# Stacked query tiles of two attention mixers: one split over all 128 rows and transfers, where before each half was split on its own rows

## The chip, the cores and the metric

One core of one Trainium2 chip runs the whole program. The metric is the device time of one execution in microseconds (us). The kernel before takes 2039.87 us (median of three runs, 2039.81 to 2040.88).

## What is computed

A trunk of two layers over 512 positions of width 1024. Each layer is: half a SwiGLU step, a mixer, half a SwiGLU step, and a gated per-layer input. All products are made in a split form: a float32 value x is written as hi + lo, where hi is x rounded to TensorE's float32r and lo = x - hi, and three products (hi hi, hi lo, lo hi) are summed.

The mixer of layer 0 is `ab`, that of layer 1 is `c`. Cut to what matters here:

```python
# layer 0: A = windowed attention, 12 heads on 4 key heads; B = dilated attention, 12 heads
oa, _ = banded_attention(rope(qa), rope(ka), va, 128, sink)
ob = dilated_attention(rope(qb), rope(kb), vb)
h = h + concat([oa, ob]) @ w_out
# layer 1: 16 heads over an 8 x 16 neighbourhood of a grid, with a learned bias
h = h + neighbourhood_attention(q, k, v, rpb) @ w_out
```

## The kernel before

**Layout.** Features lie on the 128 rows (partitions), positions on the 512 columns. Heads are 64 wide, so a chunk of 128 projected features holds two heads: `hf` 0 on rows 0 to 63 and `hf` 1 on rows 64 to 127. The tiles in question come from a pool `act` of 62 buffers of 128 x 512 (L59, L83).

**Stacked tiles.** So that one product sums over 128 rows where a head has only 64, each head gets a tile of its own: its hi part on its own 64 rows and its lo part on the other 64 (`stack_q`, L573), against a key tile that holds the key's hi part on both halves (`stack_k`, L585: ScalarE copies hi to the head's own rows, L592, SyncE's queue moves it to the other rows by a transfer within SBUF, L593, and the lo part goes to a second tile, `low`, L595). For queries, ScalarE copies the head's 64 rows (L580) and VectorE subtracts on the same 64 rows and writes the other 64 (L581): four instructions of 64 rows for a chunk of two heads, and no transfer.

**Mixer `ab`** (L753). Chunks of queries and keys are projected, rotated (`rope`, L710: VectorE at L727 and L728, then four accumulating transfers from GpSimd's queue, L731) and then stacked: six chunks `("aq", gp, j)` of A with gp 0 or 1, and two chunks `("bq", sp, 0)` of B. Scores are made at L744 (and L958 for the other groups of B), reduced at L745 and L962. **Mixer `c`** (L1061): `proj_q` (L1089) projects a chunk, scales it (L1100), stacks it, and then SyncE's queue moves the hi part of each head to a third kind of tile, `sel` (L1104); `proj_k` (L1106) follows with L1110 and `stack_k`; scores are made at L1168. The first score product of a head pair needs the stacked query, `sel`, the stacked key and `low`.

**Order of the work.** `weave` (L853) interleaves the attention steps with the projections in the order of the program text; the tile framework's planner then lays down a fixed order for each engine by program order, priorities and its own estimates. An engine, and SyncE's queue too, takes its instructions strictly in that order: a transfer that waits for its source holds back those behind it. On SyncE's queue lie the weight loads (L167), the bias loads of `c` (L1092) and the transfers named above. `split_chunk` (L877) is the plain split: hi on ScalarE (L150), lo on VectorE (L151), each over all 128 rows, into two tiles of `act`. Lines 150 and 151 belong to a helper that also splits weights (`wh`, `wl`) and transposed probabilities (`tmp`).

Of the kernel before, what the change touches and what calls it, by code (L numbers as in the profile page):

```python
# [9 lines left out]
F32 = mybir.dt.float32  # L10
F32R = mybir.dt.float32r
BF16 = mybir.dt.bfloat16
AF = mybir.ActivationFunctionType
ALU = mybir.AluOpType
# [34 lines left out]
class Trunk:  # L49
# [520 lines left out]
        self.mm_unit(p, u, self.xg, True, True)  # L570
        return p

    def stack_q(self, q):  # L573

        nc = self.nc
        out = []
        for hf in range(2):
            own, oth = slice(hf * HD, (hf + 1) * HD), slice((1 - hf) * HD, (2 - hf) * HD)
            t = self.act(F32R)
            nc.scalar.activation(t[own, :], q[own, :], AF.Copy)  # L580
            nc.vector.tensor_tensor(t[oth, :], q[own, :], t[own, :].bitcast(F32), op=ALU.subtract)  # L581
            out.append(t)
        return out

# [168 lines left out]
    def ab(self, k_next):  # L753
        nc, io = self.nc, self.io
# [23 lines left out]
        t = {}  # L778
# [4 lines left out]
        def stacked(key, i, kind, p=None):  # L783

            c = []

            def stack():
                if key[0][1] == "k":
                    low = self.lows()
                    t[key] = (self.stack_k(c[0], low), low)  # L790
                else:
                    t[key] = self.stack_q(c[0])

            return [(key + (0,), 1, lambda: c.append(self.rope(p or self.project(w[i]), kind))), (key, 0, stack)]

# [638 lines left out]
```

## Time and profile before

| | us |
|---|---|
| median of three runs | 2039.87 |
| the profiled execution | 2041.7 |
| its span, first to last instruction | 2039.8 |
| TensorE (PE) busy | 2018.5 (99%) |
| VectorE (DVE) busy | 1510.8 (74%) |
| ScalarE (ACT) busy | 1056.6 (52%) |
| GpSimd (POOL) busy | 269.2 (13%) |

The profiled execution is 1.8 us over the median. `ab`'s attention lies at about 390 to 625 us of the span, `c`'s at about 1405 to 1600 us. PE is TensorE's matmuls, PEld its weight loads, SPq SyncE's queue. A matmul's end is modelled: rows of neighbouring matmuls overlap, and the starts tell their pace.

### The profile page before, as it was taken

To read this page: it belongs to the slowest core of one execution; us is meant where nothing else is said; L and a number is where in the kernel's file an instruction comes from. 1 tells how busy PE (TensorE), PEld (TensorE's weight loads), DVE (VectorE), ACT (ScalarE), POOL (GpSimd) and SP (SyncE) were. 2 spreads that over 40 slices of the span, in tenths; PEclk is the share of its full clock that TensorE was granted. 3 is DMA by queue.
4 is the path that set the end of the run, shared out by engine and by line. 5 is a ranking of instruction groups with operands and counts; after the bars stand their busy time and mean duration, and the time that the engine had idled before them with its cause. 6 is when DMAs were issued, how large, how long until landed. Compare 5 with 4: busy or idle time off the path is not lost.

```text
span 2039.8 us, 33724 instructions
## 1 busy us (share of the span) xinstructions
PE 2018.5 (99%) x12862; PEld 1820.6 (89%) x12862; DVE 1510.8 (74%) x2575; ACT 1056.6 (52%) x1798; POOL 269.2 (13%) x306
## 2 busy tenths in 40 slices
PE   9999999999999999999999999999999999999998
PEld 6999988878888899988888999888888889998886
DVE  8888865598766888875568888755778688888554
ACT  6555543377644555553445555434666545555342
POOL 1100011342212110001211100021000111000111
PEclk9999999999999999999999999999999999999999
DMA  7776644543424477653545765545333446665451
GB/s 222 192 187 184 186 142 159 143 98 73 100 72 165 134 197 183 170 191 123 184 152 154 197 182 158 191 143 154 110 104 110 155 127 188 184 180 164 132 204 42
DMA packets 122354, 312.93 MB, mean 153 GB/s; under 512 B 23504, under 2 KB 31184, under 8 KB 122192
## 3 DMA queue, kind: packets, MB, share of 16 engines
q1 hardware_dynamic: 102336, 249.91, 37.6%
q0 software_dynamic: 19712, 60.83, 15.4%
q8 instruction: 101, 1.65, 0.3%
q14 instruction: 61, 0.50, 0.1%
q10 hardware_dynamic: 144, 0.04, 0.0%
HBM read 274.02 MB, written 25.66 MB: 147 GB/s over the span
## 4 chain that ended last, share of the span: by engine, by line
PE 90%; DVE 3%; DMA 2%; ACT 2%; issue 1%; POOL 1%; SPq 0%; DVEq 0%; POOLq 0%; ACTq 0%
PE mm L365 6%; PE mm L364 6%; PE mm L363 6%; PE mm L176 6%; PE mm L177 6%; PE mm L175 6%; PE mm L440 5%; PE mm L441 5%; PE mm L442 5%; PE sc L364 3%; PE sc L363 3%; PE sc L365 3%; PE sc L175 3%; PE sc L177 3%; PE sc L176 3%; PE ob L365 2%
## 5 line engine op out<-in xcount | busy, mean ns | idle before, releaser
L150 ACT ACTIVATE wh<-wr 128x1024 fp32r<-128x1024 f32 (+2 forms) x455 | 465.6, 1026 | 533.6 <-PE mm L441 162.6
L151 DVE TENSOR_TENSOR wl<-wr,wh 128x1024 fp32r<-128x1024 f32 (+2 forms) x455 | 538.3, 1187 | 193.5 <-ACT wh L150 189.9
L365 PE MATMUL mm<-act,wl 128*128 128x256 f32 x1088 | 307.9, 283 | 0.0
L364 PE MATMUL mm<-act,wh 128*128 128x256 f32 x1088 | 307.9, 283 | 0.0
L363 PE MATMUL mm<-act,wh 128*128 128x256 f32 x1088 | 307.9, 283 | 0.0
L175 PE MATMUL mm<-act,wh 128*128 128x512 f32 (+1 forms) x648 | 254.0, 393 | 1.0 <-ACT wh L150 0.5
L176 PE MATMUL mm<-act,wh 128*128 128x512 f32 (+1 forms) x648 | 254.1, 392 | 0.6 <-DVE act L202 0.6
L177 PE MATMUL mm<-act,wl 128*128 128x512 f32 (+1 forms) x648 | 253.7, 392 | 0.0
L364 PEld LDWEIGHTS mm<-act,wh 128*128 128x128 f32 x1088 | 208.8, 192 | 0.3
L363 PEld LDWEIGHTS mm<-act,wh 128*128 128x128 f32 x1088 | 208.9, 192 | 0.2
L365 PEld LDWEIGHTS mm<-act,wl 128*128 128x128 f32 x1088 | 208.9, 192 | 0.2
L440 PE MATMUL mm<-act,wh 128*128 128x512 f32 x512 | 199.4, 389 | 0.0
L441 PE MATMUL mm<-act,wh 128*128 128x512 f32 x512 | 199.4, 389 | 0.0
L442 PE MATMUL mm<-act,wl 128*128 128x512 f32 x512 | 199.2, 389 | 0.0
L150 ACT ACTIVATE act<-tmp 128x512 fp32r<-128x512 f32 (+1 forms) x204 | 113.9, 590 | 85.5 <-DVE tmp L524 36.8
L363 PE MATMUL sc<-act,wh 128*128 128x256 f32 x544 | 154.0, 283 | 0.0
L364 PE MATMUL sc<-act,wh 128*128 128x256 f32 x544 | 154.0, 283 | 0.0
L365 PE MATMUL sc<-act,wl 128*128 128x256 f32 x544 | 154.0, 283 | 0.0
L176 PEld LDWEIGHTS mm<-act,wh 128*128 128x128 f32 x648 | 122.2, 189 | 24.7 <-DVE act L202 2.0
L175 PEld LDWEIGHTS mm<-act,wh 128*128 128x128 f32 x648 | 122.2, 189 | 23.8 <-ACT wh L150 1.0
L177 PEld LDWEIGHTS mm<-act,wl 128*128 128x128 f32 x648 | 122.2, 189 | 22.0 <-DVE wl L151 0.2
L151 DVE TENSOR_TENSOR act<-tmp,act 128x512 fp32r<-128x512 f32 (+1 forms) x200 | 125.4, 641 | 10.4 <-ACT act L150 8.8
(225 smaller groups left out, 4431.7 us busy)
## 6 DMA issues: line engine op xcount, KB each, us to landing
wr<-in_gu_dram SPq DMA_DIRECT2D x176, 512.0 KB, 4.6
wr<-in_gu_dram POOLq DMA_DIRECT2D x68, 512.0 KB, 5.5
wr<-in_dn_dram SPq DMA_DIRECT2D x64, 512.0 KB, 3.9
rb<-in_gu_dram SPq DMA_DIRECT2D x68, 256.0 KB, 2.9
wr<-in_dn_dram SPq DMA_DIRECT2D x32, 384.0 KB, 3.3
wr<-in_qk_ab_dram SPq DMA_DIRECT2D x20, 512.0 KB, 3.5
inner<-tmp POOLq DMA_DIRECT2D x32, 256.0 KB, 3.1
tmp<-inner SPq DMA_DIRECT2D x32, 256.0 KB, 4.4
```

Source lines behind the costliest of these rows:

```text
L150: self.put(self.nc.scalar.activation(hi, src, AF.Copy))
L151: self.put((lo_eng or self.nc.vector).tensor_tensor(lo, src, hi.bitcast(F32), op=ALU.subtract))
L175: mm(out, stat[0], mov[0], start=start, stop=False)
L176: mm(out, stat[0], mov[1], start=False, stop=False)
L177: return mm(out, stat[1], mov[0], start=False, stop=stop)
L363: mm(out, w[0][:, c], xs[k][0][:, x], start=start and k == 0, stop=False, skip_group_check=True)
L364: mm(out, w[0][:, c], xs[k][1][:, x], start=False, stop=False, skip_group_check=True)
L365: mm(out, w[1][:, c], xs[k][0][:, x], start=False, stop=stop and k == half - 1, skip_group_check=True)
L440: mm(p, u[0][:, c], xh, start=start and j == 0, stop=False, skip_group_check=True)
L441: mm(p, u[0][:, c], xl, start=False, stop=False, skip_group_check=True)
L442: mm(p, u[1][:, c], xh, start=False, stop=s + j == NF - 1, skip_group_check=True)
```

## The change

`stack_q` gets a flag, which is true for all chunks except the three `("aq", 0, j)`. With it, the chunk is split once by `split_chunk` (lo on VectorE) into two tiles of 128 rows, and for each of its two heads two transfers on SyncE's queue put the head's 64 rows of hi on its own rows of the stacked tile and its 64 rows of lo on the other rows. It holds for 3 chunks of A, 2 of B and 8 of `c`.

```diff
-    def stack_q(self, q):
+    def stack_q(self, q, moved=True):
...
-        nc = self.nc
-        out = []
+        nc, out = self.nc, []
+        parts = self.split_chunk(q, nc.vector) if moved else None
         for hf in range(2):
             own, oth = slice(hf * HD, (hf + 1) * HD), slice((1 - hf) * HD, (2 - hf) * HD)
             t = self.act(F32R)
-            nc.scalar.activation(t[own, :], q[own, :], AF.Copy)
-            nc.vector.tensor_tensor(t[oth, :], q[own, :], t[own, :].bitcast(F32), op=ALU.subtract)
+            if moved:
+                for rows, x in zip((own, oth), parts):
+                    nc.sync.dma_start(t[rows, :].bitcast(F32), x[own, :].bitcast(F32))
+            else:
+                nc.scalar.activation(t[own, :], q[own, :], AF.Copy)
+                nc.vector.tensor_tensor(t[oth, :], q[own, :], t[own, :].bitcast(F32), op=ALU.subtract)
             out.append(t)
...
-                    t[key] = self.stack_q(c[0])
+
+                    t[key] = self.stack_q(c[0], key[:2] != ("aq", 0))
```

## Rows read from the trace of the kernel before

**Rows 1.** The page's first part: busy time of each engine over the span, its share, and its instructions.
```profile
PE 2018.5 (99%) x12862; PEld 1820.6 (89%) x12862; DVE 1510.8 (74%) x2575; ACT 1056.6 (52%) x1798; POOL 269.2 (13%) x306
```

**Rows 2.** Busy time by stretches: the stretch, its length, then busy us (and instructions) of PE, PEld, DVE, ACT and POOL, the granted clock, the mean share of the DMA engines, GB/s. Two stretches of A, then 200 us of each mixer.
```profile
420.00:440.00 20.00, 19.90 (x102) 16.55 (x102) 19.33 (x49) 14.48 (x35) 7.05 (x9) 1.00 0.61 127
440.00:460.00 20.00, 19.34 (x101) 15.29 (x100) 19.35 (x45) 14.53 (x32) 8.27 (x12) 1.00 0.45 93
...
400.00:600.00 200.00, 196.18 (x1170) 165.78 (x1169) 162.73 (x422) 134.63 (x333) 53.72 (x71) 0.99 0.41 87
1400.00:1600.00 200.00, 197.72 (x1228) 174.94 (x1228) 147.35 (x404) 124.59 (x277) 6.39 (x8) 1.00 0.35 101
```

**Rows 3.** The chain of work that ended last, 420 to 462 us, in order of time: start, us, engine, tile and line.
```profile
427.29 0.70 DVE act L581
...
428.27 0.69 DVE act L581
...
432.80 0.62 ACT act L580
...
433.44 0.63 ACT act L580
...
434.53 0.39 PE ob L673
...
445.15 0.69 DVE act L581
...
446.46 0.69 DVE act L581
...
457.58 0.24 PE sc L744 x2
```

**Rows 4.** Groups by line and shape, 400 to 600 us: busy us, mean ns of one, idle time before and what ended it.
```profile
L581 DVE TENSOR_TENSOR act<-act,act 64x512 fp32r<-64x512 f32 x14 | 9.6, 686 | 0.5
...
L580 ACT ACTIVATE act<-act 64x512 fp32r<-64x512 f32 x13 | 8.1, 623 | 0.2
...
L151 DVE TENSOR_TENSOR act<-act,act 128x512 fp32r<-128x512 f32 x7 | 4.8, 686 | 0.2
L150 ACT ACTIVATE act<-act 128x512 fp32r<-128x512 f32 x7 | 4.4, 622 | 0.0
```

**Rows 5.** The same view, 1400 to 1600 us.
```profile
L581 DVE TENSOR_TENSOR act<-tmp,act 64x512 fp32r<-64x512 f32 x16 | 11.3, 705 | 1.1 <-ACT act L580 0.7
...
L151 DVE TENSOR_TENSOR act<-act,act 128x512 fp32r<-128x512 f32 x8 | 5.4, 677 | 1.4 <-ACT act L150 1.4
```

**Rows 6.** DVE in order of time, 544 to 552 us.
```profile
547.68 0.69 DVE L581 TENSOR_TENSOR act<-act,act 64x512 fp32r<-64x512 f32 x1
548.40 0.56 DVE L745 CUSTOM_DVE_ANT_0 act<-sc,act 128x384 f32<-128x384 f32 x1
```

**Rows 7.** PE in order of time, 548 to 550 us; in brackets the idle time before and what ended it.
```profile
549.02 1.20 PE L958 MATMUL sc<-act,act 64*128 64x128 f32 x8 [0.24 <-DVE st_b L745]
```

**Rows 8.** The chain of work that ended last, 544 to 556 us.
```profile
554.64 0.43 PE mm L176
...
555.40 0.23 PE mm L175
```

**Rows 9.** The view of rows 2 for the four microseconds around rows 8.
```profile
552.00:556.00 4.00, 4.00 (x13) 3.24 (x13) 3.24 (x15) 1.57 (x6) 0.36 (x1) 0.60 0.29 112
```

**Rows 10.** DVE in order of time: the end of the scaling of the query chunks 2, 4 and 6 of `c` (start, us, three instructions together).
```profile
1445.93 0.81 DVE L1100 SCALAR_TENSOR_TENSOR tmp<-mm,R 128x256 f32<-128x256 f32 x3
...
1492.45 0.81 DVE L1100 SCALAR_TENSOR_TENSOR tmp<-mm,R 128x256 f32<-128x256 f32 x3
...
1538.85 0.81 DVE L1100 SCALAR_TENSOR_TENSOR tmp<-mm,R 128x256 f32<-128x256 f32 x3
```

**Rows 11.** SyncE's queue in order of time for the same three chunks: start of the issue, us that the issues took, line, transfer, count.
```profile
1451.23 1.12 SPq L593 DMA_DIRECT2D act<-act  x2
...
1493.95 1.12 SPq L1104 DMA_DIRECT2D act<-act  x2
1495.16 0.54 SPq L167 DMA_DIRECT2D wr<-in_v_c_dram  x1
1497.09 1.12 SPq L593 DMA_DIRECT2D act<-act  x2
...
1540.35 1.12 SPq L1104 DMA_DIRECT2D act<-act  x2
...
1543.49 1.12 SPq L593 DMA_DIRECT2D act<-act  x2
```

**Rows 12.** PE in order of time: the first scores of the head pairs 2, 4 and 6.
```profile
1454.18 0.40 PE L1168 MATMUL sc<-act,act 128*128 128x256 f32 x2
...
1500.73 0.36 PE L1168 MATMUL sc<-act,act 128*128 128x256 f32 x1 [0.29 <-DMA act<-act]
...
1546.68 0.28 PE L1168 MATMUL sc<-act,act 128*128 128x256 f32 x1
```

**Rows 13.** From the views of line 593 (24 transfers) and of line 1104 (16 transfers): us from issue to landing, 128 KB each.
```profile
DMA to landing us min/median/max: 2.2/2.3/5.1
...
DMA to landing us min/median/max: 2.2/2.2/2.3
```

**Rows 14.** The chain of work that ended last, 1380 to 1640 us: the key's transfer of chunk 4.
```profile
1497.09 3.50 DMA act<-act
```

## The prediction

> **What bounds the kernel now.** I read the page's engine part first: PE is busy 2018.5 us of a span of 2039.8 us [rows 1], so no other engine can bound the whole, and the change leaves PE's products as they are. What it can move is PE's waits, and only in the mixers, so I took the stretches next. In 200 us of `ab` PE is idle 200 - 196.18 = 3.8 us, in 200 us of `c` 200 - 197.72 = 2.3 us [rows 2]. These are lower bounds of what can be gained, since a matmul's modelled end hides short gaps, but they set the scale: some 6 us in 2040.
>
> Who is late differs. In A, from 420 to 460 us, DVE is busy 19.33 and 19.35 us of each 20 [rows 2], and the chain of waits runs through DVE rather than PE: the reader finds the subtractions of `stack_q` there four times (0.70, 0.69, 0.69 and 0.69 us) and its ScalarE copies twice (0.62 and 0.63 us), these just ahead of the product at 434.53 us [rows 3]. In `c` DVE and ACT are busy 147 and 125 us of 200 [rows 2], and the one wait I found beside the queries' path is that for the key's transfer [rows 12, 14].
>
> **The change part by part.**
>
> *The split.* A chunk costs today two copies of 623 ns on ACT and two subtractions of 686 ns on DVE, each over 64 rows; the same operations over 128 rows take 622 and 686 ns [rows 4]. So each changed chunk saves about 0.62 us of ACT and 0.69 us of DVE; in `c` the subtraction goes from 2 x 705 to 677 ns, 0.73 us [rows 5]. Over 5 chunks in `ab` that is 3.4 us of DVE and 3.1 us of ACT, over 8 in `c` 5.9 us of DVE.
>
> What of it lies on the path: in A two chunks have both subtractions on the chain, 2.77 us, of which half stays: 1.4 us gained. The third has both copies there, 1.25 us, half stays: 0.6 us. In B the second subtraction of the last chunk ends at 548.37 us, the score reduction that follows it starts at 548.40 us [rows 6], and PE waits 0.24 us for that reduction [rows 7]: with the subtraction gone, that wait goes, 0.2 us. Next late there is PE itself, so no more comes of it. Sum for `ab`: 2.2 us gained. The bounds: nothing, if the next wait lies right behind, and 3.4 us, if all of DVE's saving is handed on.
>
> In `c` I take nothing for the saved work: PE runs through its instructions while DVE and ACT have slack [rows 2]. The bound is the 2.3 us that PE is idle there.
>
> *The transfers in `ab`.* 5 x 4 = 20 transfers of 128 KB, each issued in about 0.56 us (a pair takes 1.12 us [rows 11]) and landed 2.2 to 2.3 us later, at most 5.1 us [rows 13]. The chunk ready at 428.96 us is first used by the fourth pair of heads, whose scores are running at 457.58 us [rows 3]; four issues and one landing, 2.2 + 2.3 = 4.5 us, or 7.3 us with the longest landing, are covered by more than 20 us. Cost nothing. If that cover were gone, it would be those 4.5 to 7.3 us once for each of five chunks. What is queued behind the waiting transfers on SyncE's queue are weight loads; I price that at nothing in `ab`, from zero to the 2.3 us of one landing.
>
> *The transfers in `c`.* Here the path is short, and this is the cost. Take T as the end of the scaling of chunk 4: 1492.45 + 0.81 = 1493.26 us [rows 10]. Today the two `sel` transfers are issued from T + 0.69 on, a weight load follows at 1495.16 (T + 1.90), and the queue is free at T + 2.4; the key's first transfer becomes issuable at 1497.09 = T + 3.83 [rows 11], and the head pair's first score product starts at 1500.73 = T + 7.47, 0.29 us late, waiting for that transfer [rows 12], which took 3.50 us [rows 14]. With the change the queue has six transfers for the queries, each a pace of 0.6 to 0.65 us (1495.16 - 1493.95 = 1.21 for two), from the end of the hi copy at T + 0.69: until T + 4.5. The two `sel` transfers must also wait for a landing: T + 0.69 + 2.2 = T + 2.9, which is inside that time. With the weight load, 0.6 us, the queue is free at T + 5.1. So the key's first transfer, needed at T + 3.83, goes out 0.7 us late if the weight load is laid behind it, 1.3 us late if not; PE, already waiting there, loses all of it. Chunk 6 has the same distance (1543.49 - 1539.66 = 3.83 us), its scores start at 1546.68, and a landing of 2.3 us after 1543.49 leaves 0.9 us of slack: it loses 0 to 0.4 us. Chunk 2 has 1451.23 - 1446.74 = 4.49 us and 1454.18 - 1453.53 = 0.65 us of slack [rows 10 to 12]: 0 us. The other chunks have a longer distance to their key and I charge them nothing. Sum: 0.7 to 1.7 us lost, and I take 1.0 us, nearer the lower end, since the planner can lay the weight load behind the key.
>
> *Buffers and data.* Each changed chunk holds two more of the 62 `act` tiles for a few microseconds. By my count from the code `c` fills about 45 of 62, and `ab` is fuller; a wait there would fall on chunks that are used much later, so nothing, with the 2.3 to 5.1 us of a landing as the other end for one chunk. 13 x 4 x 128 KB = 6.8 MB are added to DMA engines that are busy 0.41 and 0.35 of the time [rows 2]: nothing.
>
> *A rule that speaks against it.* The pair of transfers that `stack_k` issues 0.6 us apart, each on 64 rows, land 2.2 to 2.3 us after their own issue at the median [rows 13], so their landings are no further apart than their issues. The Trainium skill (DMA: Bandwidth & Descriptors, Rules for kernel authors) says that two transfers to disjoint halves of the partitions serialize, and to use one of 128 partitions instead. If that held for the whole transfer, the six would take 6 x 2.2 us, and the sum would be that of the serial rival below; the rows speak for overlapped ones.
>
> **The sum.** -2.2 + 1.0 = -1.2 us. The profiled execution takes 2041.7 us around its span of 2039.8 us, so it would become 2040.5; against the median of 2039.87, which lies 1.8 us lower, 2038.7 us.
>
> **The rivals.**
>
> *More comes through (faster).* At 552 to 556 us the granted clock averages 0.60, between its levels of 1.2 and 2.4 GHz [rows 9], and matmuls of 512 columns follow each other by 0.43 us instead of 0.23 us [rows 8]; about seven of them make 1.5 us. Just before lie score products of 64 rows and the wait of 0.24 us [rows 7]. If the shorter subtraction closes that wait and the clock stays up, and DVE's 3.4 us are all handed on, with nothing lost in `c`: -3.4 - 1.5 - 0.2 = -5.1 us, 2034.8 us. For it: DVE is full in A. Against: it needs both, and PE's visible idle time in `ab` is 3.8 us in all.
>
> *The queue holds back the keys (slower).* One mechanism: SyncE's queue takes the `sel` transfers only when the hi transfers have landed, and the key's transfers stand behind them. If landings in that bunch take 3.5 us, as chunk 4's key did [rows 14], rather than 2.2, the first `sel` goes out at T + 4.2, the second 0.65 later, the weight load ends at T + 5.5, and the key lands at T + 5.5 + 3.5 = T + 9.0, against scores at T + 7.0 to T + 7.5 [rows 12]: 1.5 to 2 us for each of chunks 2, 4 and 6, and by the same longer landings some 0.6 us for four more: about 8 us, less 1 us from `ab`: 2047 us. It decides from the point where the bunch's landings pass about 3 us. For it: that one key did take 3.5 us with a weight load in flight. Against: the sixteen `sel` transfers never took more than 2.3 us [rows 13].
>
> *Serial transfers.* If each 64-row transfer waited for the one before, the queries would be stacked at T + 0.7 + 13.2, the key would land at T + 16, and three heads alone would lose 8.6 to 9 us each: 26 us, 2065 us. The rows exclude nearly all of it.
>
> *It changes nothing that shows.* Other work of PE and the planner's new order take up what DVE saves and what the queue costs: 2039.9 us.
>
> **How the numbers follow.** A measurement of this kernel can tell about 0.2%, 4.1 us, from no change. Forecast (2038.7): 0.50. Nothing shows: 0.14. More comes through: 0.20. The queue holds back the keys: 0.13. Serial: 0.03. The first two lie within 0.2%, so same 0.64, faster 0.20, slower 0.16. The planner lays out every engine's order anew, which the trace of before can't show; that and the bounds above make the forecast's own range 2036 to 2042. The range for 8 in 10 reaches from the faster rival's price, 2034.8, to inside the slower one, 2044.5.
>
> **What would show it.** Right: in A, 420 to 460 us, one subtraction of 128 rows and about 0.68 us for each chunk, DVE's busy time there down by about 2 us, and PE's stretch shorter by as much; in `c`, the transfers of `stack_q` landing after 2.2 to 2.3 us, the key's transfer of chunks 4 and 6 issued about a microsecond later after T, and PE waiting some tenths longer for it. Wrong: landings above 3 us in `c` and PE waits for transfers at most head pairs (the slower rival), the granted clock at 1.00 throughout 540 to 560 us and a gain above 4 us (the faster one), or PE waits in `ab` for a weight load that stands behind a query's transfer.

## The result, and the profile after

The kernel after the change takes 2043.88 us (median of 22 executions, 2041.33 to 2045.64), the kernel before 2040.41 us (22 executions, 2039.81 to 2042.52). The ratio is 1.0014, with a 95% interval of 1.0008 to 1.0020: a little slower, and more than the measurement's spread. The forecast was a little faster.

In the kernel after, lines lie lower: the transfers of `stack_q` are line 583, the splits over all rows run on the helper's lines 150 and 151, a product with the transposes is 678 (before: 673), a V product 639 (634), rope 732 and 733 (727, 728), the rotation transfers 736 (731), the scores 749 (744), the key's transfer 598 (593), `sel` 1110 (1104), the scaling in `c` 1106 (1100). In the kernels of the experiments they shift by a few lines more; tile and engine tell what is meant.

The page's first part, which answers to [rows 1]:

```profile
PE 2016.1 (99%) x12862; PEld 1820.0 (89%) x12862; DVE 1501.2 (74%) x2562; ACT 1049.0 (51%) x1785; POOL 269.8 (13%) x306
```

DVE does 1510.8 - 1501.2 = 9.6 us less work than before and ACT 7.6 us less, as the split promised. PE's busy time fell by 2.4 us as well, though its products are the same: the profiled execution of before holds a stretch at half clock [rows 9], and this one does not (the same four microseconds):

```profile
552.00:556.00 4.00, 4.00 (x31) 3.40 (x29) 2.62 (x13) 2.36 (x9) 0.00 (x0) 1.00 0.86 215
```

So the two profiled executions can't be set against each other by their ends: that of after is its shortest (2041.33 us, span 2039.5), that of before (2041.7 us) lies above its median. What can be compared is where PE waits. First the stretches of [rows 2]:

```profile
420.00:440.00 20.00, 17.61 (x91) 14.79 (x90) 16.26 (x45) 11.54 (x30) 6.41 (x9) 1.00 0.73 172
440.00:460.00 20.00, 19.67 (x100) 15.46 (x99) 16.76 (x37) 13.60 (x30) 7.33 (x10) 1.00 0.53 107
400.00:600.00 200.00, 192.86 (x1163) 163.69 (x1162) 158.16 (x417) 129.81 (x323) 53.84 (x70) 1.00 0.45 100
1400.00:1600.00 200.00, 199.20 (x1237) 176.43 (x1236) 142.82 (x397) 120.22 (x269) 7.52 (x9) 1.00 0.45 124
```

PE is idle 7.1 us of 200 in `ab` where it was 3.8, and 0.8 us in `c` where it was 2.3. In A, from 420 to 440 us, DVE is busy 16.3 us and no longer 19.3, yet PE is idle 2.4 us and no longer 0.1. The view of PE's waits names them (what PE waited for: us in total, times, longest). Before, 380 to 640 us, the four longest:

```profile
PE sc L744 <- DVE st_a L745: 0.9, 1, 0.9
PE tr L663 <- DVE act L933: 0.8, 2, 0.6
PE mm L634 <- DVE act L728: 0.6, 1, 0.6
PE sc L744 <- DVE st_b L745: 0.5, 1, 0.5
```

After, the same stretch:

```profile
PE ob L678 <- ACT tmp L150: 2.4, 1, 2.4
PE mm L639 <- DVE act L733: 2.1, 2, 1.5
PE sc L749 <- DVE st_a L750: 0.8, 1, 0.8
PE sc L749 <- DVE st_b L750: 0.5, 1, 0.5
```

Two waits of more than 1 us are new, both in A. All rows of this view come to 3.8 us before and 7.5 us after.

**The first wait** ends at 435.80 us. ACT, in order of time:

```profile
431.50 0.38 ACT L150 ACTIVATE tmp<-tr 128x256 fp32r<-128x256 f32 x1 [0.49 <-PE tr L668]
434.74 0.63 ACT L150 ACTIVATE act<-act 128x512 fp32r<-128x512 f32 x1 [2.86 <-DMA act<-tmp]
435.28 0.47 ACT L150 ACTIVATE tmp<-tr 128x384 fp32r<-128x384 f32 x1
```

The middle row is the new split of a chunk over all rows. It stands in ACT's order ahead of the copy that PE waits for, and ACT sits idle 2.86 us before it, because one of the chunk's four rotation transfers has not landed. The chain of waits has that transfer:

```profile
427.01 1.50 POOL act L736 x2
428.51 6.12 DMA act<-tmp
...
434.74 0.63 ACT act L150
435.37 0.38 ACT tmp L150
```

6.12 us for 64 KB. The same four transfers in the kernel before were issued from 427.65 to 429.15 us and landed so (issue to landing):

```profile
DMA to landing us min/median/max: 2.4/3.0/3.4
```

There ACT came to its two 64-row copies at 432.80 us [rows 3], when all of them had landed, the last at 432.53. SyncE's queue of the kernel after (start, us that the issues took):

```profile
425.09 0.33 SPq L167 DMA_DIRECT2D wr<-in_v_ab_dram  x1
425.64 3.81 SPq L583 DMA_DIRECT2D act<-act  x4
429.55 0.53 SPq L167 DMA_DIRECT2D wr<-in_v_ab_dram  x1
```

Four stacking transfers of 128 KB, and behind them a weight load of 512 KB, issued 1.04 us after the last rotation transfer. Before, that load went out at 431.10 us, 1.95 us after it. Ahead of each of the two loads DVE ends a subtraction from the buffers of the weights, first before, then after:

```profile
429.82 1.22 DVE L151 TENSOR_TENSOR wl<-wr,wh 128x1024 fp32r<-128x1024 f32 x1
```
```profile
427.26 1.22 DVE L151 TENSOR_TENSOR wl<-wr,wh 128x1024 fp32r<-128x1024 f32 x1
```

**The second wait** ends at 475.63 us. PE and then DVE, in order of time:

```profile
475.63 0.39 PE L639 MATMUL mm<-wh,act 128*128 128x256 f32 x1 [1.47 <-DVE act L733]
```
```profile
472.37 0.42 DVE L151 TENSOR_TENSOR tmp<-tr,tmp 128x256 fp32r<-128x256 f32 x1 [0.88 <-ACT tmp L150]
472.71 1.99 DVE L732 TENSOR_TENSOR tmp<-mm,act 128x512 f32<-128x512 f32 x2
474.53 1.04 DVE L733 TENSOR_TENSOR act<-mm,act 128x512 f32<-128x512 f32 x1
```

PE wants a PSUM bank for the V projection. Rope's products (732, 733) still read it, since they stand in DVE's order behind the low part of a transpose that PE made late. Before, the same products came at 469.44 and 471.28 us and V started at 472.59 without a wait.

**In `c`** the view of PE's waits has these rows before, 1400 to 1640 us:

```profile
PE ob L673 <- ACT tmp L150: 1.7, 7, 0.3
PE tr L223 <- DVE ssq L216: 0.3, 1, 0.3
PE sc L1168 <- DMA act<-act: 0.3, 1, 0.3
```

and this one after:

```profile
PE ob L678 <- ACT tmp L150: 0.8, 4, 0.2
```

The change gains there: the wait for the key's transfer is gone, and the copies of the transposes come to PE sooner. SyncE's queue behaved much as forecast, chunk 4:

```profile
1494.49 2.65 SPq L583 DMA_DIRECT2D act<-act  x4
1497.25 1.98 SPq L1110 DMA_DIRECT2D act<-act  x1
1499.32 0.55 SPq L598 DMA_DIRECT2D act<-act  x1
```

The scaling of that chunk ends at T = 1493.80 us (1492.98 + 0.82), so the key's first transfer goes out at T + 5.5, 1.7 us later than before [rows 10, 11] (forecast: T + 5.1). But the head pair's first scores stand at 1502.93 us, T + 9.1 and no longer T + 7.47: PE does other work first, and waits for nothing. The stacking transfers land after these times, in `c` and then in `ab` (issue to landing):

```profile
DMA to landing us min/median/max: 2.2/2.3/4.2
```
```profile
DMA to landing us min/median/max: 2.2/3.6/5.1
```

### The profile page after: what moved, and what is told of

The parts are those of the page before. It is cut to its first block, busy times and chain, and to the rows that moved or that the text cites. A ratio compares the mean times of both kernels' runs of the same rounds, so it can differ in the third digit from the quotient of the medians.

```text
span 2039.5 us, 33803 instructions
## 1 busy us (share of the span) xinstructions
PE 2016.1 (99%) x12862; PEld 1820.0 (89%) x12862; DVE 1501.2 (74%) x2562; ACT 1049.0 (51%) x1785; POOL 269.8 (13%) x306
## 4 chain that ended last, share of the span: by engine, by line
PE 74%; DVE 2%; ACT 2%; DMA 1%; issue 1%; POOL 1%; SPq 0%; DVEq 0%; POOLq 0%; ACTq 0%
PE mm L176 6%; PE mm L175 6%; PE mm L177 5%; PE mm L365 5%; PE mm L364 5%; PE mm L363 5%; PE mm L440 4%; PE mm L441 4%; PE mm L442 4%; PE sc L365 2%; PE sc L364 2%; PE sc L363 2%; PE sc L175 2%; PE sc L177 2%; PE sc L176 2%; PE mm L639 1%
## 5 line engine op out<-in xcount | busy, mean ns | idle before, releaser
L150 ACT ACTIVATE act<-tmp 128x512 fp32r<-128x512 f32 (+1 forms) x212 | 118.9, 592 | 89.0 <-DVE tmp L524 35.3
L151 DVE TENSOR_TENSOR act<-tmp,act 128x512 fp32r<-128x512 f32 (+1 forms) x208 | 131.4, 645 | 11.2 <-ACT act L150 9.7
```

The source lines that it names most:

```text
L150: self.put(self.nc.scalar.activation(hi, src, AF.Copy))
L151: self.put((lo_eng or self.nc.vector).tensor_tensor(lo, src, hi.bitcast(F32), op=ALU.subtract))
```

## The experiments

Theory one: `c` gains, A loses, and A's loss is the two waits. Theory two, from the slower rival: `c`'s key queue loses, and A/B gain. Four kernels ran beside the kernel before (2041.15 us, 29 executions).

**again** is the changed kernel without an edit.

> The changed kernel once more, unaltered, beside its parts on one chip. Its 22 runs lay between 2041.3 and 2045.6 us, and its one profile shows the fastest of them, with no stretch at half clock around 550 us. Theory 1 (the loss is two waits of PE in A, at 436 and 476 us, and in most runs a stretch at half clock behind them): again about 2043.9 us, and a profile of a slower run shows the same two waits and a mean granted clock below 1.00 somewhere in 380 to 640 us. Theory 2 (the loss is in c, keys held back behind the queries' transfers): the two waits in A cost nothing that the time shows, and a slower run shows longer waits for transfers at the scores of c.

2043.44 us, ratio 1.0011 (1.0002 to 1.0020). Of the executions at a mean granted clock of 0.998, five of this kernel average 2043.1 us and twenty of the kernel before 2040.8 us: 2.3 us apart. PE's waits differ by about as much: in `ab` and `c` they are 3.8 + 2.3 us before, 7.5 + 0.8 us in the changed kernel's first profile and 8.2 + 0.8 us in this one, so 2.2 and 2.9 us more. The first wait is 3.3 us here, where it was 2.4: with the same order on every engine its size changes from one execution to the next.

**c_only, b_only, a_only** keep the change in one stage:

```diff
-                    t[key] = self.stack_q(c[0], key[:2] != ("aq", 0))
+                    t[key] = self.stack_q(c[0], False)
...
-            qk["q", hp] = self.stack_q(q)
+            qk["q", hp] = self.stack_q(q, False)
```

The first edit alone is c_only. The other two have the second edit, and in place of the first `key[0] == "bq"` (b_only) or `key[:2] == ("aq", 1)` (a_only) as the second argument.

> Only the eight chunks of c take the transfers; all of A and B are split as before. Theory 1: faster than before by 1 to 2 us (2038.5 to 2039.5 us against 2040.4), as the trace after shows PE's excess in c smaller by 1.8 us. Theory 2: all of the loss, about 2043.5 us.

2038.97 us, ratio 0.9988 (0.9979 to 0.9997): faster.

> Only the two chunks of B take the transfers. Theory 1: within 1 us of before, 2039.5 to 2041.5 us, perhaps 1 us less if the wait at 549 us and the stretch at half clock behind it go. Theory 2: the same, 2040.4 us.

2039.52 us, ratio 0.9995 (0.9986 to 1.0004): no difference that shows.

> Only the three chunks of A with gp 1 take the transfers. Theory 1: the whole loss and more, 2043 to 2046 us, with PE waiting over 2 us near 436 us behind ScalarE, which waits for the last rotation transfer. Theory 2: no loss, 2038 to 2040.5 us.

2046.84 us, ratio 1.0027 (1.0016 to 1.0038): slower by 5.7 us, with both waits (3.0 and 1.9 us). In c_only, `c`'s waits are the same single row of 0.8 us as in the whole change, and neither of A's new waits is there. Theory two fell: the loss is all A's. The medians of a_only and c_only, +5.7 and -2.2 us, come to the +3.5 us of the whole change's first runs; beside these kernels, in again, it was +2.3.

That leaves A. Its change has two halves, the single split and the transfers, and each could delay the rotation or reorder the engines. Four kernels beside the kernel before (2040.34 us, 27 executions).

**bc**, the change without A:

```diff
-                    t[key] = self.stack_q(c[0], key[:2] != ("aq", 0))
+                    t[key] = self.stack_q(c[0], key[0] == "bq")
```

> The change kept in B and c and taken back in A (both groups of A split on 64 rows as before). If the parts add up, as measured singly (b_only 1.6 us under the kernel before, c_only 2.2 us under it), this is 3.8 us under the kernel before: a ratio of 0.998, no PE wait at 436 or 476 us, and PE idle in 1400:1640 near 0.8 us. If B and c gain through the same cover (or B's gain was only noise), it lies at 0.9985 to 0.999.

2038.03 us, ratio 0.9990 (0.9981 to 0.9999): 2.3 us under the kernel before, where the whole change was 2.3 and 3.5 us over it. It beats both. The parts add up to less than the 3.8 us hoped for: it is c_only's gain, and B adds nothing that shows.

**a_parts**, the single split without transfers, in A's second group alone; the two parts stand in for the stacked tiles:

```diff
...
+        if moved:
+            return self.split_chunk(q, nc.vector)
```

> Only A's second group changed, and of it only the split: one Copy and one subtraction over 128 rows, no transfers; the two parts stand in for the stacked tiles, so this group's scores are of other operands (work left out: the 12 transfers). The order on ACT still has the split of a chunk ahead of the copies of the transposes that PE waits for. If the loss of a_only (+5.7 us) is the order alone (a split that waits for all four rotations, ahead of work that PE needs), the waits at 436 and 476 us are here too, 2 to 3.5 us the first, and the time is 4 to 6 us over the kernel before. If it is the transfers beside the rotation, the four rotations land 2.5 to 3.4 us after their issue as before, the first wait is under 1 us, and the time is within 1.5 us of the kernel before or below it.

2042.42 us, ratio 1.0009 (1.0001 to 1.0018): 2.1 us slower. The four rotation transfers and the wait that came of them:

```profile
DMA to landing us min/median/max: 2.4/3.3/5.0
```
```profile
PE ob L675 <- ACT tmp L150: 1.3, 1, 1.3
```

This is neither expectation: the last rotation transfer takes 5.0 us though no stacking transfer is there.

**a_dummy**, the transfers without the single split, in A's second group alone: the 64-row split as before, and twelve transfers into tiles that nobody reads. The orders of ACT and POOL are those of the kernel before, DVE's all but the same; PE's has some small moves from 430 us on.

```diff
+        spare = [self.act(F32R), self.act(F32R)] if moved else None
...
             nc.vector.tensor_tensor(t[oth, :], q[own, :], t[own, :].bitcast(F32), op=ALU.subtract)
+            if moved:
+                for rows in (own, oth):
+                    nc.sync.dma_start(spare[hf][rows, :].bitcast(F32), t[rows, :].bitcast(F32))
```

> A as before (splits on 64 rows, stacked tiles complete by them), and beside it the same 12 transfers of 128 KB from SyncE's queue in A's second group, into spare tiles that nobody reads. ACT's, DVE's and POOL's orders are those of the kernel before. If the transfers are the loss, it is here: rotations that land 4 to 6 us after issue, a PE wait of 1.5 us or more near 435 us, 3 to 5 us over the kernel before. If the order is the loss, the time is within 1 us of the kernel before, though the rotations may land late.

2043.23 us, ratio 1.0013 (1.0005 to 1.0022): 2.9 us slower, and the first wait is there, 2.6 us, with the old order. Its chain of waits:

```profile
428.25 1.50 POOL act L735 x2
429.74 7.02 DMA act<-tmp
...
436.85 0.63 ACT act L581
```

This profile has one more wait that the kernel before lacks, 1.3 us at 399.9 us for the transfer of a key; it comes before the first of the twelve transfers, issued at 426.75 us, and so is none of their doing.

**a_pool**, a_only with the transfers on GpSimd's queue:

```diff
-                    nc.sync.dma_start(t[rows, :].bitcast(F32), x[own, :].bitcast(F32))
+                    nc.gpsimd.dma_start(t[rows, :].bitcast(F32), x[own, :].bitcast(F32))
```

> As a_only, with the 12 transfers issued on GpSimd's queue in place of SyncE's, so that no weight load stands behind them. In ACT's order the split of the second chunk now stands behind all four copies of the transposes. If the held weight loads or the split's place ahead of the copies is the loss, the first wait (436 us) is gone, and the time is 2 to 4 us under a_only; if the transfers' traffic beside the rotation is, it stays within 1 us of a_only. GpSimd's issues (about 0.5 us each by the rotation's rows) may also put the next rotation later.

2053.01 us, ratio 1.0063 (1.0051 to 1.0076). The first wait is gone, but the next rotation stands behind the stacking transfers on GpSimd's queue, PE waits 1.8 us and then 2.3 us for rope's products, and the clock falls to its lower level twice (the view of rows 2):

```profile
450.00:460.00 10.00, 8.69 (x37) 7.19 (x38) 5.88 (x13) 5.49 (x15) 8.18 (x12) 0.83 0.62 109
...
480.00:490.00 10.00, 9.46 (x56) 9.35 (x56) 7.27 (x27) 3.93 (x13) 6.29 (x8) 0.72 0.46 52
```

PE's waits in `ab` and `c` explain 4.5 us of the 12.7. At 709 us PE waits 2.0 us for ACT, where neither the kernel before nor a_only waits, and the clock falls a third time, from 711 to 715 us. The mean granted clock of its executions is 0.994, that of the kernel before beside it 0.998; at the lower level a product takes 0.43 us instead of 0.23 [rows 8], so an estimate for the clock is 0.004 x 2040 = 8 us. The three terms are more than enough for the 12.7 us. As a test of the load's queue it is worthless, since it changed too much.

**A third theory.** Put side by side, the slow rotations have one thing in common, and it is not the stacking transfers. The last rotation transfer of the chunk and the 512-KB weight load that follows it (us; landing as issue plus the landing time of the view by line):

| kernel | rotation issued, landed (took) | load issued, landed |
|---|---|---|
| before | 429.15, 432.53 (3.4) | 431.10, 434.8 |
| c_only | 428.76, 432.15 (3.4) | 430.71, 434.3 |
| b_only | 429.04, 432.41 (3.4) | 430.99, 434.6 |
| bc | 429.58, 432.98 (3.4) | 431.53, 435.3 |
| after | 428.51, 434.63 (6.1) | 429.55, 435.7 |
| again | 428.87, 435.92 (7.0) | 429.78, 435.7 |
| a_only | 432.33, 439.10 (6.8) | 433.30, 438.9 |
| a_parts | 431.70, 436.7 (5.0) | 432.56, 436.4 |
| a_dummy | 429.74, 436.77 (7.0) | 430.84, 436.6 |
| a_pool | 429.59, 434.94 (5.4) | 429.62, 434.4 |

Wherever in these rows the load is issued 1.1 us or less behind the rotation transfer, the transfer takes 5.0 to 7.0 us and lands from 1.1 us ahead of the load's end to 0.5 us behind it; where it is issued 1.95 us behind, the transfer takes 3.4 us, and no run lies between. a_parts has no stacking transfers, and in a_pool they are issued only after the load. So I held the load: a transfer of 512 B on SyncE's queue reads the rotated chunk, and the load is put behind it. All engines but SyncE keep their orders exactly. Four kernels beside the kernel before (2040.32 us, 33 executions).

```diff
+                    if key == ("aq", 1, 1):
+                        self.gate = nc.sync.dma_start(self.spare[96:, :], c[0][96:, 0:4])
...
-            u = self.unit(src[:, q * UNIT:(q + 1) * UNIT], lo_eng=self.lo_eng())
+            with self.tc.issue_after(self.gate.ins) if self.gate and not parts else ExitStack():
+                u = self.unit(src[:, q * UNIT:(q + 1) * UNIT], lo_eng=self.lo_eng())
+            if not parts:
+                self.gate = None
```

**whole_held**, on the whole change:

> The whole change, and one transfer of 512 B more on SyncE's queue, which reads the rotated second chunk of A's second group, so that the 512-KB weight load behind it is issued only when the rotation has landed; the orders of all engines are else those of the whole change. If that load, issued about a microsecond behind the last rotation transfer, is what makes this transfer land with it (434.64 against 435.71 us in the whole change, a_parts 436.66 against 436.43, a_dummy 436.77 against 436.59), the fourth rotation transfer lands within 4.3 us of its issue, the wait at 436 us falls from 2.4 us to under 0.7, and the kernel is 2 to 3 us faster than the whole change, so 2040.5 to 2041.5 here and within 0.1% of the kernel before. If the stacking transfers themselves are what slows the rotation, the wait stays over 2 us and the time at 2043 to 2044. The wait at 476 us stays in both cases.

2041.00 us, ratio 1.0003 (0.9994 to 1.0012). The rotation lands in 4.1 us at most, and the wait at 436 us falls from 2.4 us to 0.4:

```profile
DMA to landing us min/median/max: 3.0/4.0/4.1
```
```profile
PE ob L681 <- ACT tmp L150: 0.4, 1, 0.4
```

The hold moves the meeting to the next rotation, whose last transfer takes 9.4 us, and no longer 6.0 as in the kernel after. PE waits 1.5 us there, at 444 us (the second row), and the second wait stays (the first):

```profile
PE mm L642 <- DVE act L736: 2.1, 2, 1.5
PE ob L682 <- DVE tmp L151: 1.8, 2, 1.5
```

**a_parts_held**, on a_parts:

> a_parts (A's second group split over all rows, no transfers, other operands in its scores) with the same hold on the weight load. If the load is the cause, the fourth rotation transfer lands about 3.4 us after its issue as in the kernel before, not 5.0, the wait of 1.5 us near 437 us is gone, and the time is 1 to 2 us under a_parts, within 0.5 us of the kernel before or below it. If the split's standing for all four rotations is enough by itself, the wait stays at 1 us or more and the time at a_parts'.

2039.79 us, ratio 0.9997 (0.9988 to 1.0006), 2.6 us under a_parts, directly and against the kernels before beside the two. The wait is gone and the rotation lands as before:

```profile
DMA to landing us min/median/max: 2.4/3.0/3.4
```

**a_only_held**, on a_only:

> a_only with the same hold. If the load is the cause, the wait near 440 us falls from 3.2 us to under 0.7 and the time is 2.5 to 3 us under a_only, 2 to 3.5 us over the kernel before, of which 2.1 us is the wait at 480 us. If the stacking transfers are, it stays within 1 us of a_only.

2044.18 us, ratio 1.0020 (1.0011 to 1.0029), 2.7 us under a_only. Against the kernel before beside each, it is +3.9 where a_only was +5.7: 1.8 us less, short of the 2.5 expected, and over the 3.5 us that it was to stay within. The rotation lands in 4.4 us at most, the first wait is 0.6 us, the second stays at 1.9.

**before_held**, the control:

> The kernel before with the same hold: the control. Its load was issued 1.95 us after the last rotation transfer and 1.4 us ahead of its landing, so the hold puts it back by about 1.5 us. Both theories: within 0.5 us of the kernel before, no new PE wait.

2040.04 us, ratio 0.9998 (0.9989 to 1.0007), no new wait. The third theory holds for the first wait: in all three pairs it goes, or nearly, with the orders of PE, DVE, ACT and POOL untouched. In the times the intervals of each pair overlap, but all three fell against the kernel before, by 1.6 to 2.8 us (the whole change from +2.3 or +3.5 to +0.7). The load's place behind the rotation costs 1.6 us (a_parts) to 2.4 us (a_only: 6.8 against 4.4) of landing; with the stacking transfers and no load behind it, it takes 0.7 to 1.0 us longer than without them (4.1 and 4.4 us against 3.4). With the load held A still costs 3.9 us, and of the first wait only 0.6 us is left in that.

The second wait occurs in every kernel whose A has both the single split and the transfers (longest 1.5 us in after, again and whole_held, 1.9 in a_only and a_only_held, 2.3 in a_pool) and in none with one half alone (a_parts, a_dummy: 0.6 us, as before). To see whether it is the bank, ACT copies that projection, and no other, out and rope reads the copy (beside the kernel before at 2040.66 us, 27 executions).

```diff
+        if free:
+            own = self.act()
+            with self.tc.high_priority():
+                nc.scalar.activation(own, p, AF.Copy)
+            p = own
         o, u = self.act(), self.tmp()
```

**a_rope**, on a_only_held:

> a_only_held with one thing more: the bank of the projection whose rope products PE waited for at 476 us is copied out by ACT (one Copy of 128x512, about 0.6 us), and the rope products read the copy, so that PE's V projection no longer waits for DVE. If that bank is the second wait, it falls from 1.9 us to under 0.5 and the kernel is 1.5 to 2.5 us faster than a_only_held (2044.2), 1 to 2.5 us over the kernel before. If something else that comes with the transfers holds PE there, a wait of 1.5 us or more stays at that place and the time stays within 1 us of a_only_held.

2043.52 us, ratio 1.0015 (1.0006 to 1.0024). The wait is gone: the V projection starts like this in a_only_held and then in a_rope,

```profile
475.59 0.38 PE L642 MATMUL mm<-wh,act 128*128 128x256 f32 x1 [1.91 <-DVE act L736]
```
```profile
474.49 0.28 PE L642 MATMUL mm<-wh,act 128*128 128x256 f32 x1
```

but the time fell by only 0.7 us (1.0 against the kernels before beside the two), short of the 1.5 to 2.5 expected. The copy also changed the orders of PE, DVE and ACT, and other waits took the place of the one that went: those in `ab` come to 6.3 us, in a_only_held to 6.4.

**before_rope**, the control:

> The kernel before with the same copy on ACT, the control: its V projection started without a wait at 472.6 us, so there is nothing to win. Within 0.5 us of the kernel before, up to 1 us slower if ACT's 0.6 us falls on the chain.

2041.62 us, ratio 1.0004 (0.9995 to 1.0013). The copy itself brings a new order, with more waits for DVE: the rows of `ab` come to 6.0 us, not 3.8, led by

```profile
PE sc L749 <- DVE st_b L750: 1.8, 3, 0.7
PE tr L663 <- DVE act L938: 1.2, 2, 0.6
```

Against this control a_rope is 1.9 us slower, where a_only_held is 4.1 us slower than its own (before_held). That fits a second wait of about 2 us, but the edit was not clean enough to price it.

**whole_rope**, on whole_held:

> whole_held with the same copy: the whole change without both of its waits in A. If these two waits are all of the loss and c's 1.3 us and B's gain stay, it is 1.5 to 2 us under whole_held, at 2038.5 to 2039.5 us, on the faster side of the kernel before by 1 to 2 us, and no better than bc (2038.0). If the 1.6-us wait that whole_held has newly at 444 us (the next rotation beside the held load) stays as well, 2039.5 to 2040.5.

2040.05 us, ratio 0.9999 (0.9990 to 1.0008). The 1.4-us wait at 444 us stays. Without the second wait and with 0.4 us left of the first, the change is even with the kernel before, and bc is still the better kernel.

The sums of the view of PE's waits against the medians, each as the difference to the kernel before (waits: `ab` 3.8, `c` 2.3 us):

| kernel | waits in `ab` | in `c` | together, against before | median, against before |
|---|---|---|---|---|
| c_only | 3.6 | 0.8 | -1.7 | -2.2 |
| b_only | 4.0 | 1.7 | -0.4 | -1.6 |
| bc | 4.1 | 0.8 | -1.2 | -2.3 |
| after | 7.5 | 0.8 | +2.2 | +3.5 |
| again | 8.2 | 0.8 | +2.9 | +2.3 |
| a_only | 8.5 | 2.0 | +4.4 | +5.7 |
| a_parts | 5.5 | 2.2 | +1.6 | +2.1 |
| a_dummy | 6.6 | 1.7 | +2.2 | +2.9 |
| a_parts_held | 4.4 | 1.9 | +0.2 | -0.5 |
| a_only_held | 6.4 | 2.2 | +2.5 | +3.9 |
| whole_held | 6.5 | 0.8 | +1.2 | +0.7 |
| before_held | 3.7 | 2.2 | -0.2 | -0.3 |
| a_rope | 6.3 | 2.0 | +2.2 | +2.9 |
| before_rope | 6.0 | 2.7 | +2.6 | +1.0 |
| whole_rope | 5.8 | 1.1 | +0.8 | -0.6 |
| a_pool | 8.5 | 2.1 | +4.5 | +12.7 |

Without a_pool they agree within about 1.6 us. That is as large as some of the differences, so the table ranks the kernels and does not price each wait.

## Why the prediction was wrong

**The step that failed: "The transfers in `ab` ... Cost nothing", and with it "What is queued behind the waiting transfers on SyncE's queue are weight loads; I price that at nothing in `ab`".** I asked who waits for a load that comes late, and nobody does. I did not ask beside what a load runs that goes out at another moment. The load goes out after a subtraction on DVE that reads the buffers of the weights: that ended at 431.04 us before and ends at 428.48 us after, ahead of the rotation's last issue, and the four stacking transfers in the queue hold the load until 429.55. So it goes out 1.0 us behind the last rotation transfer and no longer 1.95, and that transfer lands after 6.1 us and not 3.4. ACT's split, which waits for it, stands ahead of a copy that PE needs: 2.4 us. The hold left 0.6 us or less of this wait and brought the medians, against the kernel before, from +3.5 (+2.3 in again) to +0.7 us (the whole change), from +2.1 to -0.5 (a_parts) and from +5.7 to +3.9 (a_only). The trace of before showed the mechanism already, one rotation further on, where nobody needed it: the four transfers issued from 433.2 to 434.7 us, beside a load issued at 434.41, took

```profile
DMA to landing us min/median/max: 2.4/5.8/6.3
```

In a_dummy, where the load after the same rotation goes out at 438.05 us, 2.5 us behind its last transfer, the four took 3.1 to 3.6 us.

"6.8 MB are added to DMA engines ... nothing" was wrong as well, by 0.7 to 1.0 us on the same landing.

**The order of the engines.** "The planner lays out every engine's order anew, which the trace of before can't show" stood among the uncertainties with no price of its own. With it came the second wait, 1.5 to 2 us. That PE waits there for rope's products is in the trace, and in a_rope, where they read a copy, PE no longer waits there. What the wait costs is not shown, since the copy changed the orders too; what made the planner put that transpose later only where both halves of the change meet was not tried and stays open.

**A and B's gain of 2.2 us did not come.** The step read two subtractions on the chain of waits as time PE would get back. a_parts_held has the single split, no transfers and no PE wait for a rotation, and is within 0.5 us of the kernel before, with 4.4 us of waits where there were 3.8. A chain may run through DVE while PE, the bound, is hardly idle: from 420 to 460 us PE was busy 19.90 and 19.34 us of each 20 [rows 2], so the trace of before had 0.8 us to gain there, and 2.0 were forecast. In B the wait of 0.24 us did go, but one of 0.2 us came at another product: b_only has 4.0 us of waits in `ab` against 3.8, and its median can't be told from that of the kernel before.

**In `c` both terms had the wrong effect.** "I take nothing for the saved work" missed a gain: PE's waits for ACT's copies of the transposes, 1.7 of the 2.3 us before, fell to 0.8 us. The prediction named the wait for the key's transfer alone there, which is 0.3 us. That the saved work did this, and not the new order, no run shows. The 1.0 us for the key was sized from the queue, and the queue was right (chunk 4's key 1.7 us later, chunk 6's 1.8: 1545.05 against a T of 1538.57 + 0.81), but the new order put the scores later, so no PE wait came of it. Sum in `c`: 1.5 us gained by the waits (a median of -2.2 us in c_only), where 1.0 us lost was forecast.

**The rivals.** "The queue holds back the keys" had a right point, that landings stretch when a load is in flight, in the wrong stage: in `c` they did reach 4.2 us, with nobody waiting. "Serial transfers" did not happen; the median landing in `c` is 2.3 us. "More comes through" had its clock stretch gone, but so it was in c_only, which leaves A and B alone and whose engines have the order of the kernel before until 1400 us. So it comes in some executions and not in others, and the rival's subtraction was not what closed it.

**Landing beside a load.** In again, a_only, a_parts and a_dummy a 64-KB transfer, issued first, lands about 0.2 us after the 512-KB load behind it; in the first profile of the kernel after it lands 1.1 us ahead of it. The Trainium skill (DMA: Bandwidth & Descriptors, Queues, rings and completion order) says that each DMA engine takes turns between the queues that have work for it, a packet at a time. By turns of equal size one would expect the small transfer to be done well ahead of the load, and these rows do not show that. For pricing the measurement decides; why it is so no run here shows.

## What to carry to other kernels

A transfer that nobody waits for still has a time at which it runs: when a change makes an engine release a buffer sooner, or lengthens a queue ahead of a load, look at what else is in flight at the load's new moment, and at who waits for that. Read a gain off the idle time of the engine that bounds, not off the chain: in A, work taken from a chain that hardly left PE idle gave nothing back. And when a change goes into several stages, run it in each alone before judging it: here `c` gains 2 us, B shows nothing, and A's loss hides the gain.

## What was not expected of the hardware

A rotation transfer of 64 KB took 3.4 us with the 512-KB load held until it had landed (a_parts_held), and also with the load issued 1.95 us behind it on another queue. With the load issued 1.1 us or less behind it, it took 5.0 to 7.0 us. With stacking transfers of 128 KB beside it and the load held, it took 4.1 to 4.4 us. The stacking transfers themselves, 2.2 us at best, took 3.6 us at the median in `ab`, where rotation and loads are in flight, and 2.3 us in `c`.
